# Three edits in a recurrent layer: block transposes for a triangular inverse, a subtraction moved to GpSimd, two projections moved into a norm

## Chip, cores, metric

One NeuronCore of a Trainium2 chip. The metric is the device time of one execution in microseconds. The kernel before: 1786.72 us, median of 3 runs (1777.45 to 1789.82).

## What is computed

Four layers over 512 tokens of width 1024, in float32: an "even" layer (a 31-tap convolution beside an RWKV-7 recurrence), a sparse attention layer, a linear recurrent layer, a second attention layer. Only the even layer is edited. Its recurrence, per head of 64 channels:

```python
def rwkv7_step(state, inp):
    r_t, w_t, k_t, v_t, kk_t, a_t = inp
    sa = jnp.einsum('bhvk,bhk->bhv', state, -kk_t)
    state = (state * w_t[:, :, None, :]
             + sa[..., None] * (kk_t * a_t)[:, :, None, :]
             + v_t[..., None] * k_t[:, :, None, :])
    y = jnp.einsum('bhvk,bhk->bhv', state, r_t)
    return state, y
...
    y = ((y - mu) * lax.rsqrt(var + GN_EPS)).reshape(B, S, RWKV_DIM) * lnx_w + lnx_b
```

Before it, `z = h @ even_w_in` gives all inputs of convolution and recurrence; behind it come a norm per head (the group norm), a gate and `even_w_out`.

## The kernel before, in words

Activations lie transposed, channels on partitions, 512 tokens in the free dimension; a weight tile is 128x128. Every weight product is three matmuls (`mm3`, L166): the weight is split into a high part `wh` and a low part `wl`, the activation into two as well, and L168, L169, L170 add up high x high, high x low and low x high. The split is made in `wparts` (L141): ScalarE writes `wh` (L145) and minus the raw weight, rounded, into `wl` (L146), and an accumulating DMA, issued on GpSimd's queue, adds the raw weight (L147), which leaves the low part. `wsplit` loads and splits one column of 8 tiles; `wrows` (L150) loads, for one input row `k`, the 7 tiles of the first 7 columns, 8 times: 56 tiles. They serve the start (L495 to L506): while the conditioning weights `ada_first` are loaded and multiplied on VectorE (`Ada.columns`, L437: 8 operations of L445 and L447, a matmul L450, and L453, which ends a round), two rows of `h` at a time become ready (L501, L332, L333) and 7 columns accumulate in 7 PSUM banks.

The recurrence runs in two halves of 8 heads, `H0` and `H1`, objects of the class `Half`. `keys` and `prep` make the decayed keys and queries `AR` and `BK`. `inverse` (L658) inverts the 64x64 unit-triangular matrix of each of 8 chunks and 8 heads: L669 makes the products, L671 masks them on VectorE, L672 writes them to DRAM, L675 and L677 read blocks of 32x32 back, so that the row index lies on partitions 32 by 32 (`Nu`) or the upper right block is to hand (`No`). A solve by columns, 108 short operations (54 each of L688 and L689) on VectorE, inverts the diagonal blocks; L690 to L692 spill the result. `merge` (L696) reads it back (L703, L705) and makes the upper right block with two small matmuls per chunk and head (L714, L719). `ahead(c)` (L722) prepares the matrices of the next chunk; it is called for chunk 0 at the end of `inverse`, and its product with the decay (L745) is on GpSimd. `chunk(c)` steps through the 8 chunks and lets 8 steps of an independent projection (`fill`) run in between. `finish` (L804) is the group norm: centring matmuls L811, squares, `head_sums` (L544: L550, the reciprocal root, a transpose L556), then for each of four tiles a broadcast `head_bcast` (L561) and three VectorE operations L827 to L829.

Beside it run the convolution: `conv_in` (two projections), `taps` (27 operations L859 on VectorE, two additions L864 on GpSimd), `conv_stats` (its layer norm: 8 subtractions L888 and 7 additions L894 on GpSimd), `norm_conv`. `yb` is the first half's result, read back and split at L968 to L973 (L972 is a GpSimd subtraction) for 6 columns of `even_w_out`.

The order on each engine is fixed when the program is built: a scheduler with a cost model takes ready instructions by priority, which is the order of the calls; `K.later` lowers the priority, `issue_after(i)` holds an instruction behind `i`. Tiles of one tag share a number of buffers (`s=6`: six), and a new tile waits for the oldest's readers. The order of calls around the change (L919 to L978): `H0.keys`, `H0.prep`, `H0.inverse`, `H0.merge`, `conv_in(3)`, gate projections, `conv_in(4)`, `H1.keys`, the 8 chunks of H0, `H0.finish`, `taps(6)`, `H1.prep` (whose first loop turn projects H1's first `r` and `v`, L613 and L614), `H1.inverse`, later `conv_stats`, `yb`, `norm_conv`, then `H1.merge`.

Of the kernel before, what the change touches and what calls it, by code (L numbers as in the profile page):

```python
# [52 lines left out]
class Ctx:  # L53
# [87 lines left out]
    def wparts(self, raw, tag=None):  # L141

        nc, n = self.nc, raw.shape[1]
        h, l = ((self.t(tag, (P, 4, P), R) if tag else self.wp.tile([P, 4, P], R, name=self.name(z), tag=z, bufs=4))[:, :n] for z in ("wh", "wl"))
        nc.scalar.copy(h, raw)  # L145
        nc.scalar.mul(l, raw, -1.0)  # L146
        nc.gpsimd.dma_start(out=l, in_=raw, accum_op=OP.add)  # L147
        return h, l

    def wrows(self, key, ct, k):  # L150
# [6 lines left out]
        for o in (0, 4):  # L157
            m = min(4, n - o)
            h, l = self.wparts(raw[:, o:o + m])
# [300 lines left out]
def even_layer(K, ada1):  # L460
# [12 lines left out]
    with K.layer("even", {"mm": (0, 1), "t": (2, 3, 4), "u": (5, 6), "ada": (7,), "py": (7,)}, s=6, k=4, v=4, q4=3, no=1, Yt=1, BKt=2, SAV=2, U=3, cu=2, fg=3, mean=2, awa=1, pa=1):  # L473
# [70 lines left out]
        def head_sums(sqs, f, n=S):  # L544
# [21 lines left out]
        class Half:  # L566
# [91 lines left out]
            def inverse(self):  # L658
# [3 lines left out]
                No, Nu = K.t("no", (P, 4 * NCH, 32)), K.t("q4", (P, 32, 32))  # L662
                n = K.name("sp")
                nd = K.dram.tile([P, 4 * NCH, C], F, name=n, tag=n)
                for j in range(4):
# [4 lines left out]
                    n = K.t(shape=(P, NCH, C))  # L670
# [7 lines left out]
                Yu, pr = K.t("q4", (P, 32, 32)), K.t("q4", (P, 32, 32))  # L678
# [984 lines left out]
```

## Time and profile before

| what | us |
|---|---|
| median of 3 runs | 1786.72 |
| the profiled execution | 1791.05 |
| its span | 1789.3 |
| PE busy in the span | 1657.9 |
| VectorE (DVE), ScalarE (ACT), GpSimd (POOL) busy | 1142.2, 1090.4, 637.6 |

Engines: PE is TensorE's matmuls, PEld its weight loads, SP the queue that issues most DMAs. A group of instructions is told by its line. "Idle before" is the time its engine did nothing, and behind the arrow stands what ended it. [...]

### The profile page before, as it was taken

Reading aid. Unit: us, or ns where it says so; the run is one execution under the profiler, and the core shown is the slowest. Engines: PE = TensorE matmul, PEld = TensorE weight load, DVE = VectorE, ACT = ScalarE, POOL = GpSimd, SP = SyncE. Lnnn points to the kernel's source line nnn. Section 1 sums busy time; section 2 is a strip of 40 time slices with the busy share of each in tenths; the row PEclk is TensorE's granted clock in tenths of the full one; section 3 lists DMA queues with packets and bytes.
Section 4 is the critical chain, followed back from the end, with each engine's and each line's share of the span. In section 5 each row is a group of like instructions: output and inputs, shape, how many; then the busy total and the mean of one; then the engine's idle time right before and its main releaser. Section 6 shows DMA issues by size and latency. Waiting matters only on the chain.

```text
span 1789.3 us, 26544 instructions
## 1 busy us (share of the span) xinstructions
PE 1657.9 (93%) x9250; PEld 1310.1 (73%) x9250; DVE 1142.2 (64%) x2247; ACT 1090.4 (61%) x2106; POOL 637.6 (36%) x678
## 2 busy tenths in 40 slices
PE   5899999998995999888999899999999999999997
PEld 4676777776664777767887688888788777877775
DVE  6489776795948567456968878922688621454442
ACT  3574545445554435478565678765789755776775
POOL 1244423233566212133323445332333333333332
PEclk9899997898998989899999999999999999999999
DMA  9866894446678976476879741078777798865654
GB/s 284 211 147 163 184 215 110 107 95 174 153 179 193 273 219 151 119 170 142 179 168 229 197 89 35 18 166 193 165 177 167 150 190 190 199 143 138 154 109 116
DMA packets 164087, 289.19 MB, mean 162 GB/s; under 512 B 43985, under 2 KB 60753, under 8 KB 162929
## 3 DMA queue, kind: packets, MB, share of 16 engines
q0 software_dynamic: 60352, 107.24, 35.7%
q1 hardware_dynamic: 99568, 172.91, 30.9%
q10 hardware_dynamic: 4032, 7.34, 1.1%
q8 instruction: 73, 1.20, 0.3%
q14 instruction: 62, 0.50, 0.1%
HBM read 162.10 MB, written 18.12 MB: 101 GB/s over the span
## 4 chain that ended last, share of the span: by engine, by line
PE 59%; DVE 13%; DMA 12%; issue 8%; ACT 3%; POOL 3%; SPq 1%; POOLq 0%; DVEq 0%; ACTq 0%
PE ps L168 15%; PE ps L169 15%; PE ps L170 15%; DVE x L859 4%; DMA wl<-wr 3%; DMA wr<-in_even_w_in 2%; POOL wl L147 1%; DMA adm<-in_ada_w 1%; PE ps L1525 1%; PE ps L729 1%; DMA sp<-gt 1%; PE ps L1521 1%; PE ps L550 1%; PE ps L1261 1%; POOL mean L894 1%
## 5 line engine op out<-in xcount | busy, mean ns | idle before, releaser
L147 POOL DMA_DIRECT2D wl<-wr x416 | 364.7, 882 | 871.6 <-ACT wl L146 772.3
L170 PE MATMUL ps<-h,wl 128*128 128x512 f32 x1240 | 498.8, 406 | 29.4 <-DMA wl<-wr 29.0
L168 PE MATMUL ps<-h,wh 128*128 128x512 f32 x1240 | 508.5, 415 | 18.7 <-ACT h L332 6.8
L169 PE MATMUL ps<-h,wh 128*128 128x512 f32 x1240 | 500.0, 405 | 0.1
L145 ACT CAST wh<-wr 128x512 fp32r<-128x512 f32 (+1 forms) x416 | 251.9, 606 | 355.6 <-PE ps L169 253.8
L170 PEld LDWEIGHTS ps<-h,wl 128*128 128x128 f32 x1240 | 241.0, 195 | 91.0 <-DMA wl<-wr 37.5
L168 PEld LDWEIGHTS ps<-h,wh 128*128 128x128 f32 x1240 | 243.4, 197 | 83.3 <-ACT h L332 8.3
L169 PEld LDWEIGHTS ps<-h,wh 128*128 128x128 f32 x1240 | 242.0, 195 | 52.7 <-issue 2.7
L146 ACT ACTIVATE wl<-wr 128x512 fp32r<-128x512 f32 (+1 forms) x416 | 256.5, 617 | 28.0 <-PE ps L169 26.5
L859 DVE SCALAR_TENSOR_TENSOR x<-cu,vec,x 128x512 f32<-128x512 f32 x216 | 185.9, 862 | 4.9
L1258 POOL TENSOR_SCALAR pp<-pp,st 128x512 f32<-128x512 f32 x32 | 52.2, 1632 | 68.9 <-DVE st L1254 58.8
L1253 ACT ACTIVATE pp<-pp,st 128x512 f32<-128x512 f32 x64 | 46.2, 722 | 18.2 <-DVE st L1252 18.0
L1515 DVE CUSTOM_DVE_ANT_0 pp<-ps,nb 128x128 f32<-128x128 f32 (+3 forms) x64 | 30.6, 488 | 30.3 <-PE ps L1510 21.8
L169 PE MATMUL ps<-wl,h 128*128 128x512 f32 x120 | 47.6, 398 | 0.7 <-DMA wl<-wr 0.7
L1252 DVE CUSTOM_DVE_ANT_0 pp<-ps,bias 128x512 f32<-128x512 f32 x64 | 43.6, 681 | 6.4 <-PE ps L1261 6.0
L170 PE MATMUL ps<-wh,h 128*128 128x512 f32 x120 | 46.5, 393 | 0.0
L688 DVE TENSOR_TENSOR q<-q,q 128x112 f32<-128x112 f32 (+25 forms) x108 | 27.2, 288 | 29.2 <-DMA q<-sp 28.8
L168 PE MATMUL ps<-wh,h 128*128 128x512 f32 x120 | 45.4, 405 | 0.0
L288 ACT CAST pT<-ps 128x512 fp32r<-128x512 f32 x64 | 36.4, 577 | 14.1 <-PE ps L1261 13.6
L1518 POOL TENSOR_SCALAR pp<-pp,st 128x128 f32<-128x128 f32 (+1 forms) x32 | 32.0, 1032 | 36.5 <-DVE st L1517 36.4
L289 DVE TENSOR_TENSOR pT<-ps,pT 128x512 fp32r<-128x512 f32 x64 | 43.3, 680 | 0.8 <-ACT pT L288 0.7
L1188 DVE MATCH_REPLACE8 acc<-m,acc 128x512 f32<-128x512 f32 x64 | 42.8, 674 | 0.0
(522 smaller groups left out, 3332.1 us busy)
## 6 DMA issues: line engine op xcount, KB each, us to landing
wl<-wr POOLq DMA_DIRECT2D x376, 256.0 KB, 4.1
wr<-in_even_w_in SPq DMA_DIRECT2D x50, 512.0 KB, 4.1
wr<-in_odd_w_in SPq DMA_DIRECT2D x39, 512.0 KB, 4.2
wr<-in_lru_w_in SPq DMA_DIRECT2D x24, 512.0 KB, 3.8
wr<-in_fox_w_qkg SPq DMA_DIRECT2D x24, 512.0 KB, 4.4
k<-in_ada_w SPq DMA_DIRECT2D x32, 256.0 KB, 3.9
wr<-in_odd_w_out SPq DMA_DIRECT2D x16, 512.0 KB, 4.0
wl<-wr POOLq DMA_DIRECT2D x40, 192.0 KB, 4.1
```

What stands on the lines that cost most here:

```text
L145: nc.scalar.copy(h, raw)
L146: nc.scalar.mul(l, raw, -1.0)
L147: nc.gpsimd.dma_start(out=l, in_=raw, accum_op=OP.add)
L168: mm(ps, lhsT=w[0], rhs=x[0], start=first, stop=False)
L169: mm(ps, lhsT=w[0], rhs=x[1], start=False, stop=False)
L170: self.last_mm = mm(ps, lhsT=w[1], rhs=x[0], start=False, stop=last).ins
L289: nc.vector.tensor_tensor(out=l, in0=src, in1=h.bitcast(F), op=OP.subtract)
L859: nc.vector.scalar_tensor_tensor(out=acc, in0=u[:, q:q + S], scalar=w[q], in1=acc, op0=OP.mult, op1=OP.add)
L1188: nc.vector.match_replace(out=acc, in_to_replace=m8, in_values=acc, imm_value=TAKEN)
L1252: nc.vector.tensor_tensor_reduce(out=pp, in0=lg, in1=bias[t], scale=1.0, scalar=3e38, op0=OP.add, op1=OP.min, accum_out=mx)
L1253: nc.scalar.activation(pp, pp, AF.Exp, scale=-1.0, bias=mx, accum_out=sm)
L1258: (nc.vector if t % 2 else nc.gpsimd).tensor_scalar(out=pp, in0=pp, scalar1=sm, scalar2=None, op0=OP.mult)
```

## The change

`wparts` gets a flag: with it, GpSimd subtracts `wh` from the raw weight directly. Only `wrows` sets it. `inverse` keeps the unmasked products in `Yt` (ScalarE copies) and turns 32x32 blocks with VectorE's transpose, before and after the solve; no DRAM is used, `No` goes. `ahead(0)` moves from the end of `inverse` into `merge`. `ahead`'s decay product goes to four ScalarE multiplications. `conv_in(3)` is called ahead of `H0.merge`. In `H0.finish`, H1's first `r` projection is called inside `head_sums` and its first `v` projection behind it, with the transposes and broadcasts held behind their last matmuls; `H1.prep` then finds them done. L894 moves to VectorE. The split of `yb` goes the other way: from a GpSimd subtraction to ScalarE and an accumulating DMA.

```diff
     def wparts(self, raw, tag=None, sub=False):
         nc.scalar.copy(h, raw)
-        nc.scalar.mul(l, raw, -1.0)
-        nc.gpsimd.dma_start(out=l, in_=raw, accum_op=OP.add)
+        if sub:
+            nc.gpsimd.tensor_tensor(out=l, in0=raw, in1=h.bitcast(F), op=OP.subtract)
+        else:
+            nc.scalar.mul(l, raw, -1.0)
+            nc.gpsimd.dma_start(out=l, in_=raw, accum_op=OP.add)
...
-            h, l = self.wparts(raw[:, o:o + m])
+            h, l = self.wparts(raw[:, o:o + m], sub=True)
...
-        def head_sums(sqs, f, n=S):
+        def head_sums(sqs, f, n=S, behind=None):
...
+            if behind:
+                behind()
             p = K.ps("t")
-            for t in range(nt):
-                nc.tensor.transpose(p[:16, t * P:(t + 1) * P], hl[:, t].bitcast(F), K.ident)
+            with K.tc.issue_after(K.last_mm) if behind else contextlib.nullcontext():
+                for t in range(nt):
+                    nc.tensor.transpose(p[:16, t * P:(t + 1) * P], hl[:, t].bitcast(F), K.ident)
...
+                Yt = self.Yt = K.t("Yt", (P, 4 * NCH, C))
                 for j in range(4):
...
-                    nc.vector.tensor_tensor(out=n, in0=v3(p), in1=gmask[:, None, 0:C].to_broadcast([P, NCH, C]), op=OP.mult)
-                    nc.sync.dma_start(out=nd[:, NCH * j:NCH * j + NCH], in_=n)
-                quarters = [(b, q, 64 * b + 32 * q, slice(64 * q + 32 * b, 64 * q + 32 * b + 32)) for b in range(2) for q in range(2)]
-                for b, q, r, o in quarters:
-                    nc.sync.dma_start(out=Nu[o], in_=nd[r:r + 32, :, 32 * q:32 * q + 32].rearrange("a u b -> u a b"))
-                    if q == 0:
-                        nc.sync.dma_start(out=No[r:r + 32], in_=nd[r:r + 32, :, 32:64])
+                    nc.scalar.copy(Yt[:, NCH * j:NCH * j + NCH], v3(p))
+                quarters = [(q, slice(64 * b + 32 * q, 64 * b + 32 * q + 32)) for q in range(2) for b in range(2)]
+                turn = nc.vector.transpose
...
+                for q, r in [(0, slice(0, P))] + quarters[2:]:
+                    turn(out=Nu[r].rearrange("u a b -> u b a"), in_=Yt[r, :, 32 * q:32 * q + 32].rearrange("a u b -> a b u"))
...
-                Yd = K.spill(Yu)
-                self.last = nc.vector.tensor_copy(pr[0:64], Yu[0:64].rearrange("p a b -> p b a"))
-                Xd = K.spill(pr[0:64])
+                X11 = self.X11 = K.t("q4", (P, 32, 32))
+                turn(out=X11.rearrange("p u a -> p a u"), in_=Yu)
+                for q, r in quarters[2:] + [(0, slice(0, P))]:
+                    self.last = turn(out=Yt[r, :, 32 * q:32 * q + 32].rearrange("p u b -> p b u"), in_=Yu[r].rearrange("u a b -> u b a"))
+
+            def merge(self, fill=()):
...
+                for b in range(2):
+                    nc.gpsimd.memset(Yt[64 * b + 32:64 * b + 64, :, 0:32], 0.0)
                 self.ahead(0, K.t("SAV", (P, 2, 4, C)))
...
-                    nc.gpsimd.tensor_tensor(out=bk, in0=BK[:, :, c].rearrange("p j a t -> p j (a t)"), in1=pcb, op=OP.mult)
                     p = K.ps("t")
                     for j in range(4):
+                        nc.scalar.mul(bk[:, j], BK[:, j, c].rearrange("p a t -> p (a t)"), self.PC[:, j, c:c + 1])
                         nc.tensor.transpose(p[:, j * P:(j + 1) * P], bk[:, j], K.ident)
...
-                r8 = head_sums(sqs, f_gn, n)
+                r8 = head_sums(sqs, f_gn, n, behind[0])
+                if behind[1]:
+                    behind[1]()
+                after = K.last_mm if behind[1] else None
                 for j, (y, ft) in enumerate(zip(ys, self.fts)):
-                    p = head_bcast(r8, j)
+                    with K.tc.issue_after(after) if after else contextlib.nullcontext():
+                        p = head_bcast(r8, j)
...
-                    nc.gpsimd.tensor_tensor(out=acc, in0=acc, in1=sq[:, :S], op=OP.add)
+                    nc.vector.tensor_tensor(out=acc, in0=acc, in1=sq[:, :S], op=OP.add)
...
+        conv_in(3)
         H0.merge()
-        conv_in(3)
...
-        H0.finish(gates)
+        H0.finish(gates, behind=(lambda: K.project(W, [CR + 4], hT, H1.ev_r), lambda: K.project(W, [CVV + 4], hT, H1.ev_v)))
...
                 nc.scalar.copy(h, y)
-                nc.gpsimd.tensor_tensor(out=l, in0=y, in1=h.bitcast(F), op=OP.subtract)
+                nc.scalar.mul(l, y, -1.0)
+                nc.gpsimd.dma_start(out=l, in_=y, accum_op=OP.add)
```

## Rows read from the trace of the kernel before

**Rows 1.** Windows (start:end, length, busy us per engine, PEclk, DMA share, GB/s).
```profile
0.00:785.00 785.00, 688.26 (x4556) 530.51 (x4556) 551.96 (x967) 386.75 (x721) 278.38 (x296) 0.91 0.71 176
785.00:1789.00 1004.00, 969.60 (x4694) 779.56 (x4694) 590.19 (x1281) 703.61 (x1386) 359.25 (x382) 0.99 0.66 150
214.00:285.00 71.00, 64.84 (x411) 52.16 (x409) 46.08 (x144) 33.72 (x63) 21.38 (x24) 0.90 0.94 202
412.00:440.00 28.00, 23.52 (x89) 15.11 (x88) 11.47 (x18) 14.04 (x24) 4.63 (x6) 0.78 0.76 198
440.00:517.00 77.00, 69.02 (x357) 49.18 (x356) 62.80 (x80) 39.52 (x68) 40.65 (x42) 0.90 0.62 147
517.00:600.00 83.00, 64.76 (x466) 51.42 (x464) 53.21 (x134) 43.06 (x75) 51.08 (x40) 0.86 0.91 227
```

**Rows 2.** Waits of PE, 0 to 780 us (total, times, longest).
```profile
PE ps L170 <- DMA wl<-wr: 23.0, 9, 10.9
```

**Rows 3.** DMA queues, 0 to 80 us (packets, MB, share).
```profile
q1 hardware_dynamic: 11360, 17.09, 64.9%
q0 software_dynamic: 2304, 3.67, 27.0%
```

**Rows 4.** Timeline of VectorE, the first stage (start, duration, idle before).
```profile
22.95 0.16 DVE L453 TENSOR_TENSOR mod<-ps,vec 128x4 f32<-128x4 f32 x1 [1.96 <-PE ps L450]
35.66 0.16 DVE L453 TENSOR_TENSOR mod<-ps,vec 128x4 f32<-128x4 f32 x1 [3.09 <-PE ps L450]
...
70.47 0.16 DVE L453 TENSOR_TENSOR mod<-ps,vec 128x4 f32<-128x4 f32 x1 [2.56 <-PE ps L450]
```

**Rows 5.** Lines of GpSimd, 0 to 785 us (busy, mean ns, idle before).
```profile
L864 POOL TENSOR_TENSOR pa<-pa,awa 128x512 f32<-128x512 f32 x16 | 25.4, 1589 | 15.2 <-ACT awa L863 14.9
...
L745 POOL TENSOR_TENSOR s<-BK,PC 128x512 f32<-128x512 f32 x14 | 15.8, 1233 | 5.6 <-PE ps L719 5.4
L888 POOL TENSOR_TENSOR x<-x,mean 128x512 f32<-128x512 f32 x8 | 10.0, 1277 | 0.1
```

**Rows 6.** Lines of VectorE and ScalarE, 0 to 785 us.
```profile
L447 DVE SCALAR_TENSOR_TENSOR SAV<-AR,cs,SAV 128x512 f32<-128x512 f32 x14 | 10.5, 749 | 2.3 <-DMA AR<-in_ada_first 1.9
...
L904 DVE RECIPROCAL mean<-mean 128x512 f32<-128x512 f32 x1 | 3.4, 3353 | 4.6 <-ACT mean L899 4.6
...
L750 ACT COPY BKt<-ps 128x512 f32<-128x512 f32 x14 | 8.1, 580 | 4.6 <-PE ps L748 3.1 <-PE ps L790 1.3
...
L801 ACT COPY AR<-ps 128x256 f32<-128x256 f32 x16 | 6.0, 373 | 6.6 <-PE ps L800 6.5
```

**Rows 7.** Timelines of VectorE and PE, the inverse of H0.
```profile
230.29 0.28 DVE L688 TENSOR_TENSOR q<-q,q 128x31 f32<-128x31 f32 x2 [15.89 <-DMA q<-sp]
...
251.55 0.18 DVE L689 TENSOR_TENSOR q<-q,q 128x8 f32<-128x8 f32 x1
...
252.84 1.11 DVE L691 COPY q<-q 64x1024 f32<-64x1024 f32 x1
...
270.87 3.59 PE L714 MATMUL ps<-q,no 32*32 32x32 f32 x64 [3.15 <-issue]
```

**Rows 8.** Timelines of ScalarE and PE, the group norm of H0.
```profile
434.24 0.69 ACT L527 ACTIVATE s<-ps,tiny 128x512 f32<-128x512 f32 x1 [6.33 <-DVE AR L829]
...
436.78 0.79 PE L168 MATMUL ps<-h,wh 128*128 128x512 f32 x1 [2.43 <-DVE s L528]
```

**Rows 9.** Timelines of GpSimd, VectorE and PE, the inverse of H1.
```profile
511.16 9.99 POOL L888 TENSOR_TENSOR x<-x,mean 128x512 f32<-128x512 f32 x8
...
530.40 1.38 DVE L688 TENSOR_TENSOR q<-q,q 128x31 f32<-128x31 f32 x2 [12.87 <-DMA q<-sp]
...
537.26 12.65 POOL L894 TENSOR_TENSOR mean<-mean,cu 128x512 f32<-128x512 f32 x1
...
554.89 0.79 PE L170 MATMUL ps<-h,wl 128*128 128x512 f32 x1 [10.93 <-DMA wl<-wr]
...
581.38 3.59 PE L714 MATMUL ps<-q,no 32*32 32x32 f32 x64 [5.82 <-issue]
```

More of the change, by code (lines that the diff above doesn't have):

```diff
@@ L139, in wsplit, with wparts @@
         return out
-    def wparts(self, raw, tag=None):
+    def wparts(self, raw, tag=None, sub=False):
         nc, n = self.nc, raw.shape[1]
@@ L472, in even_layer @@
     A = Ada(K, 0)
-    with K.layer("even", {"mm": (0, 1), "t": (2, 3, 4), "u": (5, 6), "ada": (7,), "py": (7,)}, s=6, k=4, v=4, q4=3, no=1, Yt=1, BKt=2, SAV=2, U=3, cu=2, fg=3, mean=2, awa=1, pa=1):
+    with K.layer("even", {"mm": (0, 1), "t": (2, 3, 4), "u": (5, 6), "ada": (7,), "py": (7,)}, s=6, k=4, v=4, q4=3, Yt=1, BKt=2, SAV=2, U=3, cu=2, fg=3, mean=2, awa=1, pa=1):
         xT, hT = [], []
@@ L669, in inverse @@
                             mm(p[hs(b), c * C:(c + 1) * C], lhsT=BK[hs(b), j, c, b], rhs=AR[hs(b), j, c, 0], start=True, stop=True)
[L670 to L678 removed]
+                    nc.scalar.copy(Yt[:, NCH * j:NCH * j + NCH], v3(p))
+                quarters = [(q, slice(64 * b + 32 * q, 64 * b + 32 * q + 32)) for q in range(2) for b in range(2)]
+                turn = nc.vector.transpose
+                Nu, Yu, pr = (K.t("q4", (P, 32, 32)) for _ in range(3))
                 nc.gpsimd.memset(Yu, 0.0)
                 nc.gpsimd.memset(Yu.rearrange("p a b -> p (a b)")[:, 0::33], 1.0)
+                for q, r in [(0, slice(0, P))] + quarters[2:]:
+                    turn(out=Nu[r].rearrange("u a b -> u b a"), in_=Yt[r, :, 32 * q:32 * q + 32].rearrange("a u b -> a b u"))
                 for b in range(31):
@@ L689, in inverse @@
                             eng.tensor_tensor(out=Yu[:, a, b + 1:], in0=Yu[:, a, b + 1:], in1=z, op=OP.add)
-                Yd = K.spill(Yu)
-                self.last = nc.vector.tensor_copy(pr[0:64], Yu[0:64].rearrange("p a b -> p b a"))
-                Xd = K.spill(pr[0:64])
-                self.ahead(0, K.t("SAV", (P, 2, 4, C)))
-                self.parts = No, Yd, Xd, quarters
-            def merge(self, fill=()):
-                No, Yd, Xd, quarters = self.parts
-                Yt = self.Yt = K.t("Yt", (P, 4 * NCH, C))
-                X11 = K.t("q4", (P, 4 * NCH, 32))
-                for b, q, r, o in quarters:
-                    f = lambda d, o: d[o].rearrange("u a b -> a u b")
-                    nc.sync.dma_start(out=Yt[r:r + 32, :, 32 * q:32 * q + 32], in_=f(Yd, o))
-                    if q == 0:
-                        nc.sync.dma_start(out=X11[r:r + 32], in_=f(Xd, o))
-                    else:
-                        nc.gpsimd.memset(Yt[r:r + 32, :, 0:32], 0.0)
+                X11 = self.X11 = K.t("q4", (P, 32, 32))
[3 more added lines that the diff above has]
+            def merge(self, fill=()):
+                Yt, X11 = self.Yt, self.X11
+                for b in range(2):
+                    nc.gpsimd.memset(Yt[64 * b + 32:64 * b + 64, :, 0:32], 0.0)
+                self.ahead(0, K.t("SAV", (P, 2, 4, C)))
                 for u in range(0, 4 * NCH, 16):
@@ L713, in merge @@
                         for c in range(16):
-                            i = mm(p[r2, 32 * c:32 * c + 32], lhsT=No[r, u + c], rhs=X11[r, u + c], start=True, stop=True)
+                            i = mm(p[r2, 32 * c:32 * c + 32], lhsT=Yt[r, u + c, 32:64], rhs=X11[r, u + c], start=True, stop=True)
                         if fill:
@@ L802, in chunk, with finish @@
                 return last.ins
-            def finish(self, gate, c0=0, c1=NCH):
+            def finish(self, gate, c0=0, c1=NCH, behind=(None, None)):
                 n = (c1 - c0) * C
```

4 lines of the change are left out of this document (removed).

## Prediction

> **What bounds the kernel now.** Read the stage windows first [rows 1]. From 785 us on nothing is edited; TensorE (PE) is busy there 969.60 of 1004 us at a granted clock of 0.99, so there is nothing to win. The first 785 us are the edited layer: PE is busy 688.26 us, idle 97 us, and the mean clock is 0.91. [...] Second, the waits of PE [rows 2]: the largest sum is for `wl`, the low half of a weight, 23.0 us in nine waits. Third, the timelines, which place the rest: four places, taken in order of time.
>
> **Place 1: the first 56 weight tiles (`wrows`).** Up to 80 us the DMA engines move loads for 64.9% of the time and accumulating DMAs, which make `wl` from `wr`, for 27.0%, 21.6 us [rows 3]; together 92%. The 16 accumulating DMAs of `wrows` become 16 GpSimd subtractions, and 16 ScalarE multiplications go. The stage's pace is read at L453, which ends each of the four rounds of `Ada.columns`: the first at 22.95 us, the second at 35.66, the fourth at 70.47 [rows 4]. The first interval, 12.71 us, is a round that waits for no DMA; the other two are 17.4 on average. With the loads alone (52 us of DMA time) all intervals could be 12.71: the last round ends at 22.95 + 3 x 12.71 = 61.1, 9.4 us earlier. That is the upper end.
> What GpSimd's subtraction costs is not shown for this place; the nearest rows are its other 128x512 operations [rows 5]: 1277 ns alone (L888), 1589 ns beside the taps on VectorE (L864). Sixteen of them (half are 128x384) need about 22 us of some 50, and GpSimd has nothing else there. But both engines hold each other up: if each of the four subtractions of an interval keeps VectorE from its chain (L447, 749 ns each [rows 6]) for 1277 ns, an interval is 12.71 + 5.1 us, and the last round ends at 22.95 + 53.4 = 76.4, 5.9 us later than now. That is the lower end, -6. VectorE waits for DMA or PE in a part of each round, so I take a quarter of that delay, 1.3 us an interval: gain 9.4 - 3.9, say **5 us** (-6 to 9).
> [...]
>
> **Place 2: the inverse of the first half (H0).** Now the masked blocks go to DRAM and come back transposed: VectorE stands idle 15.89 us before the solve starts at 230.29; the solve ends at 251.7; after it a spill, a second round trip, and the merge's matmuls start at 270.87 after a PE wait of 3.15 [rows 7]. Per inverse 4 masking multiplications, 18 DMAs and a strided copy go; 4 ScalarE copies (about 0.58 us, as L750 [rows 6]) and 7 VectorE block transposes of 1024 elements per partition come: 3 before the solve, 4 after. No row shows such a transpose. Below it lies the strided copy of 1024 elements after this solve, 1.11 us (L691) [rows 7], above it the slowest VectorE operation, the reciprocal, 3353 ns for 512 elements, so 6.7 us for 1024 [rows 6]. I take 1.2 us, near the copy, since it moves and doesn't compute. So the chain from last block product to merge loses 15.89 + 19.1 = 35 us of waiting and gets 7 x 1.2 + about 1.5 for copies and memset = 10: 25 us shorter. That is not 25 us of time, because PE works on independent projections meanwhile. The window 214 to 285 has PE busy 64.84 of 71 us: 6.2 idle; its clock of 0.90 means 14 us at half speed, of which about 10 with work, 5 us of it lost [rows 1]. Ceiling 11. What is late next is the supply of independent projections, which now must also fill the earlier chunks. I take **6 us** (0 to 11). `conv_in(3)` moved ahead of the merge is such a filler: nothing.
>
> **Place 3: the group norm of H0 (`finish`).** 412 to 440 has 4.5 us idle at 0.78 [rows 1], which is 12 us at half speed; about 9 of them with work, 4.5 lost. Ceiling 9. The largest wait, 2.43 us, is for the evacuation of H1's first `r` projection, whose ScalarE half itself waited 6.33 us for the norm's last step (L829) to free a tile [rows 8]. Issued ahead of the norm's own tiles, that wait goes. But the scheduler already put one of the two projections into this stretch (4.5 of 28 us idle is all that is left), and the two that move are not extra work; `head_bcast` now queues behind 24 of their 48 matmuls on PE, and the norm's chain behind it, which only the next stage reads. I take **4 us** (0 to 9).
>
> **Place 4: the inverse of H1.** The dearest. VectorE idles 12.87 us, from 517.5 to the solve's start at 530.40. Inside it one of GpSimd's L894 holds its queue from 537.26 for 12.65 us; behind it in that queue stand the issues of `wl` DMAs, and PE idles 10.93 us for `wl` until 554.89; then 5.82 us more until the merge at 581.38 [rows 9]. The window 517 to 600: 18.2 us idle, clock 0.86, 23 us at half speed of which about 11 with work: 5.6 lost [rows 1]. Ceiling 24. The change takes L894's seven additions to VectorE (about 0.7 us each, 5 us, before or behind the solve) and the four subtractions of `yb` off GpSimd (four accumulating DMAs and four ScalarE multiplications instead), so nothing that reads SBUF should be queued on GpSimd during the solve. Left is L888, eight subtractions of 1277 ns [rows 5], which ran from 511.16 to 521.15 [rows 9] and must end before the solve begins: with three transposes after 517.5, at about 521. If they don't, the queue is blocked for the whole solve, 21.4 us (230.29 to 251.7) instead of 12.65, PE stalls 9 us longer, and only the merge wait of 6 goes: -3. I take **15 us** (-3 to 24).
>
> **The rest.** `ahead`'s product moves from GpSimd (1233 ns, L745 [rows 5]) to four ScalarE multiplications of 128 columns. From 373 ns for 256 columns and 580 for 512 [rows 6] one is about 270 ns: 1.1 us, as long as before, 15 us over 14 chunks on an engine that is busy 387 of 785 us [rows 1]. It stands ahead of the copies of U in ScalarE's queue, but PE has filler there: 0 (-3 to 3).
>
> **Sum.** 5 + 6 + 4 + 15 = 30 us. The profiled execution took 1791.05 us (span 1789.3), 4.3 above the median of 1786.72. 1791.05 - 30 = 1761, and less 4.3: **1757 us**, 1.7% under the median. About 1% (18 us, below 1769 or above 1805) is what a measurement of this kernel can tell from no change.
>
> **Rivals.**
> *A, the stall stays at H1.* L888 overlaps the earlier solve, or PE has no filler: place 4 gives 3 instead of 15, the sum is 18: 1769. For it: L888 ended at about 521, just where the solve would begin. [...]
> *B, the lock bites in the first stage.* Place 1 gives -6: sum 19, 1768. For it: VectorE's chain is the stage's pacemaker. Against: it idles in each round, and the two intervals above 12.71 were long for the DMAs that now go.
> *C, the waits come back elsewhere.* The filler is used up early or late all the same, and the preparation of H1 runs at VectorE's pace (62.80 of 77 us between 440 and 517 [rows 1]): places 2 to 4 give a third of 25, place 1 its 5: 13, so 1773. It includes that the two moved projections change nothing.
> *D, slower: a dear transpose.* At the reciprocal's rate, 6.7 us, seven of them and the 1.5 make 48.4 us, 13 more than the 35 they replace, in each inverse; PE has run out of filler there already, so both times 13 us are PE's: 26 - 5 - 4 = 17 us more, 1804. From 4.8 us a transpose the chain is no shorter; from about 5.5 the whole is slower than before.
>
> **Chances.** Forecast 0.56, A 0.14, B 0.09, C 0.14, D 0.07. Nearly all of the forecast and a part of A and B lie under 1769, so faster by over 1% has 0.63. D and what lies beyond it give slower by over 1% 0.07, and within 1% is left 0.30. The range: the four ceilings add up to 53 (1734), all at once unlikely: 1736 below; above it takes in A, B and C with some room and stops short of D: 1786.
>
> **What would show it.** In the profile after: L453's last row near 65 us, no DMA of `software_dynamic` kind before 70; VectorE's idle time before the solves under 6 us; transposes near 1.2 us; no L894 on GpSimd and no PE wait near 10 us for `wl`; waits in 412 to 440 under 2 us; window 0 to 785 ending near 755. Wrong if transposes take over 4 us, if GpSimd's subtractions in the first stage mean over 2.5 us, or if idle time of PE in the layer stays near 97 us.

## The result, and the profile after

The changed kernel takes 1758.93 us (median of 4 runs, 1758.11 to 1759.96), the kernel before 1786.72: a ratio of 0.9854 over the single runs (0.9844 by the medians), 95% interval 0.9826 to 0.9882. The forecast was 1757. The profiled execution took 1759.96 us, its span 1758.1. In the changed file the lines from L141 on stand 4 further down (L453 is L457), those of `inverse` and behind it shift a little more; all numbers below are those of the changed file unless a row of before is meant.

The windows of the changed kernel that answer to [rows 1] (PEclk is the granted TensorE clock as a share of full speed); where a stage became shorter, its window did too:

```profile
0.00:754.00 754.00, 678.54 (x4551) 523.26 (x4551) 571.68 (x974) 399.76 (x769) 249.84 (x274) 0.93 0.66 171
214.00:285.00 71.00, 68.31 (x534) 56.48 (x533) 66.20 (x159) 38.11 (x67) 21.39 (x25) 0.94 0.72 165
400.00:443.00 43.00, 39.12 (x161) 28.30 (x159) 20.97 (x30) 23.12 (x41) 12.24 (x13) 0.92 0.71 179
443.00:511.00 68.00, 57.96 (x293) 38.28 (x294) 55.50 (x66) 33.67 (x59) 37.01 (x35) 0.82 0.50 126
511.00:573.00 62.00, 57.44 (x396) 45.52 (x397) 55.04 (x139) 44.07 (x87) 20.95 (x23) 0.94 0.92 230
```

The edited layer ends 31 us earlier in the profiled execution; between the medians the gain is 28 us, as the profiled execution of before lay 4.3 us above its median and that of the changed kernel 1.0. Behind the layer, from 754 to 1758 us, TensorE works 969.16 of 1004 us, as before. In the layer TensorE's idle time fell from 97 to 75.5 us and its mean clock rose from 0.91 to 0.93. The window around the first inverse lost 3.5 us of its idle time, the one around the second inverse fell from 83 to 62 us. One row went the wrong way: the preparation of H1 (443 to 511) now has 10 us of idle time at a clock of 0.82, where it had 8 at 0.90.

TensorE's largest wait in the layer is one at its very start that the change doesn't touch (L364 for VectorE's L356, 12.8 us; 12.1 before). The rows behind it say what is late now; the 23.0 us for `wl` of [rows 2] are 8.2:

```profile
PE ps L172 <- ACT h L336: 8.9, 4, 2.7
PE ps L656 <- DVE s L651: 8.9, 3, 4.7
PE ps L174 <- DMA wl<-wr: 8.2, 7, 2.5
```

**Where the time came from, by stage.** I add up, from windows of some 4 us, TensorE's idle time and half of the time in which it worked at a granted clock of 0.50, as the prediction did for single places. TensorE is the layer's busiest engine in both kernels (688.26 of 785 us before, 678.54 of 754 after; no other is above 552 and 572). Its clock has two levels in the trace: of 1570 windows of 0.5 us in the layer of before, 1274 have 1.00, 262 have 0.50, and 34 lie between. At 0.50 its 128x512 products started every 0.43 us (298.85 to 300.99 us), at 1.00 every 0.23 (301.36 to 301.82). "Control" is a second profile of the changed kernel. The sums are estimates (they shrink by 38 and 40 us where the layer got 31 and 33 shorter), so they rank the stages and don't measure them. The border of two stages alone is worth some 4 us: cut exactly at the first and the last chunk step, H1's inverse keeps 7.8 and 7.7 us and its steps 12.3 and 12.9.

| stage | before | after | control |
|---|---|---|---|
| start and H0's keys and prep (0 to 200 us) | 43.7 | 44.0 | 40.8 |
| H0's inverse and merge | 11.6 | 7.1 | 8.1 |
| H0's eight chunk steps | 18.5 | 8.2 | 6.8 |
| group norm and H1's prep | 23.5 | 25.3 | 25.3 |
| H1's inverse and merge | 24.4 | 9.3 | 13.3 |
| H1's eight chunk steps | 18.3 | 9.8 | 6.3 |
| rest of the layer | 9.4 | 7.6 | 8.6 |
| end of the layer (last L989, L990), us | 766.1 | 734.8 | 732.7 |

Some 20 of the 38 us were lost before in the chunk steps, a stage for which the prediction's only term was the 0 of the decay product. The windows of these steps, first half and second half, of before (285 to 404, 600 to 721) and after (285 to 388, 572 to 691):

```profile
285.00:404.00 119.00, 113.72 (x1087) 91.18 (x1084) 98.20 (x139) 54.96 (x112) 43.80 (x49) 0.89 0.39 97
600.00:721.00 121.00, 111.79 (x1029) 88.63 (x1028) 81.50 (x163) 51.83 (x116) 23.02 (x29) 0.92 0.69 191
```
```profile
285.00:388.00 103.00, 99.01 (x956) 78.22 (x955) 83.97 (x124) 57.35 (x130) 35.74 (x41) 0.96 0.44 108
572.00:691.00 119.00, 112.23 (x1095) 89.30 (x1095) 84.04 (x168) 58.91 (x135) 23.84 (x30) 0.94 0.75 217
```

TensorE was nearly always busy in the first one before, too (5 us idle), but at a mean clock of 0.89. The granted clock was 0.50 for some 14 us behind a stall of 2.9 us, for some 3 us behind one of 1.9 us, and for some 10 us from 291 on without a stall ahead of it: in the 6 us before, TensorE was busy all the time, for a good part with products of 32 and of 2 columns (L719, L550). So an idle stretch stood ahead of two of these three stretches only; what lowered the clock is not shown.

**Place 1 after.** The DMA queue that made `wl` is at 0.3% instead of 27.0% of 0 to 80 us, and the subtractions cost 1.4 and 1.2 us. But the rounds end at 39.36 and 69.10, against 35.66 and 70.47 in [rows 4]. DMA queues, GpSimd's lines and the rounds:

```profile
q0 software_dynamic: 22, 0.05, 0.3%
```
```profile
L148 POOL TENSOR_TENSOR wl<-wr,wh 128x512 fp32r<-128x512 f32 x8 | 11.2, 1398 | 33.4 <-ACT wh L146 33.4
L148 POOL TENSOR_TENSOR wl<-wr,wh 128x384 fp32r<-128x384 f32 x8 | 9.9, 1234 | 2.5 <-ACT wh L146 1.3 <-PE ps L174 1.2
```
```profile
39.36 0.16 DVE L457 TENSOR_TENSOR mod<-ps,vec 128x4 f32<-128x4 f32 x1 [3.89 <-PE ps L454]
53.45 0.16 DVE L457 TENSOR_TENSOR mod<-ps,vec 128x4 f32<-128x4 f32 x1 [2.35 <-PE ps L454]
69.10 0.16 DVE L457 TENSOR_TENSOR mod<-ps,vec 128x4 f32<-128x4 f32 x1 [6.10 <-PE ps L454]
```

Each round waits for TensorE's L454, and the last one 6.10 us. (The rounds of before waited for the same products, L450, as the brackets of [rows 4] say; there the third, at 54.81, waited longest, 7.99 us, and in TensorE's queue ahead of its L450 stood products that waited 3.65 us for `wl`.) VectorE had finished the last round's sums at 63.0; L454 ran at 68.11, because it stands in TensorE's queue behind the 42 products of two rows of `h`:

```profile
57.52 5.48 DVE L451 SCALAR_TENSOR_TENSOR SAV<-BK,cs,SAV 128x512 f32<-128x512 f32 x7
```
```profile
68.11 0.95 PE L454 MATMUL ps<-ones,SAV 128*128 128x1 f32 x8
```

GpSimd and VectorE do hold each other up here. The seven operations L451 took 5.48 us in this last round, where the subtractions began only with the last of them, and 7.22 us in the round before, with two subtractions (VectorE, then GpSimd):

```profile
43.88 7.22 DVE L451 SCALAR_TENSOR_TENSOR SAV<-AR,cs,SAV 128x512 f32<-128x512 f32 x7
```
```profile
47.06 2.71 POOL L148 TENSOR_TENSOR wl<-wr,wh 128x512 fp32r<-128x512 f32 x2 [5.71 <-ACT wh L146]
```

That is 1.7 us in one round and 0.9 in another (6.39 us for the seven), about the 1.3 that the prediction took; behind TensorE's order it doesn't show in the rounds' ends.

**The inverses after.** Timelines of VectorE (three transposes before the solve, four behind it) and TensorE in H0:

```profile
210.14 6.75 DVE L683 STREAM_TRANSPOSE q<-Yt 128x1024 f32<-128x1024 f32 x3 [0.20 <-ACT Yt L676]
...
237.93 2.10 DVE L694 STREAM_TRANSPOSE q<-q 128x1024 f32<-128x1024 f32 x1
240.04 7.07 DVE L696 STREAM_TRANSPOSE Yt<-q 32x1024 f32<-32x1024 f32 x3
```
```profile
248.55 1.19 PE L710 MATMUL ps<-q,Yt 32*32 32x32 f32 x32
```

Against [rows 7] the wait before the solve (15.89 us) is gone, the solve starts at 216.9 instead of 230.29, and the merge's first product at 248.55 instead of 270.87. A transpose of 1024 elements takes 2.0 to 2.3 us, on 128 partitions as on 32. Yet the first chunk step (L777) starts at 289.2, against 287.1 before: TensorE had other work either way. In H1 (GpSimd, then VectorE):

```profile
501.15 12.58 POOL L888 TENSOR_TENSOR x<-x,mean 128x512 f32<-128x512 f32 x8
```
```profile
516.98 4.44 DVE L683 STREAM_TRANSPOSE q<-Yt 32x1024 f32<-32x1024 f32 x2
521.45 0.28 DVE L691 TENSOR_TENSOR q<-q,q 128x31 f32<-128x31 f32 x2
```

L888 ends at 513.7, 8 us before the solve; no GpSimd operation but the issuing of DMAs meets the solve, which takes 21.0 us instead of 26.9. The 12.65 us of [rows 9] and TensorE's 10.93 us behind it have no counterpart.

### The profile page after: what moved, and what is told of

Its sections match the earlier page's. It is cut to its first block, busy times and chain, and to the rows that moved or that the text cites. A ratio compares the mean times of both kernels' runs of the same rounds, so it can differ in the third digit from the quotient of the medians.

```text
span 1758.1 us, 26497 instructions
## 1 busy us (share of the span) xinstructions
PE 1647.7 (94%) x9250; PEld 1302.3 (74%) x9250; DVE 1163.9 (66%) x2258; ACT 1105.8 (63%) x2158; POOL 610.0 (35%) x657
## 4 chain that ended last, share of the span: by engine, by line
PE 64%; DVE 14%; DMA 8%; issue 7%; ACT 5%; POOL 2%; SPq 0%; POOLq 0%; ACTq 0%; DVEq 0%
PE ps L172 17%; PE ps L173 17%; PE ps L174 16%; DMA wl<-wr 3%; DVE x L859 3%; PE ps L725 1%; PE ps L1526 1%; DVE q L692 1%; DVE q L691 1%; DMA s<-sp 1%; DMA cu<-sp 1%; PE ps L1522 1%; POOL wl L151 1%; DMA adm<-in_ada_w 1%; PE ps L1262 1%
## 5 line engine op out<-in xcount | busy, mean ns | idle before, releaser
L151 POOL DMA_DIRECT2D wl<-wr x400 | 349.0, 876 | 843.4 <-ACT wl L150 731.2
L150 ACT ACTIVATE wl<-wr 128x512 fp32r<-128x512 f32 (+1 forms) x400 | 247.6, 619 | 29.5 <-PE ps L173 27.0
L859 DVE SCALAR_TENSOR_TENSOR x<-cu,vec,x 128x512 f32<-128x512 f32 x216 | 181.4, 841 | 4.7
L1254 ACT ACTIVATE pp<-pp,st 128x512 f32<-128x512 f32 x64 | 46.2, 722 | 17.6 <-DVE st L1253 17.4
L1523 ACT COPY pT<-ps 128x128 f32<-128x128 f32 (+3 forms) x64 | 25.8, 419 | 27.7 <-PE ps L1522 27.5
```

What stands on the lines that cost most here:

```text
L859: nc.vector.scalar_tensor_tensor(out=acc, in0=u[:, q:q + S], scalar=w[q], in1=acc, op0=OP.mult, op1=OP.add)
L1254: nc.scalar.activation(pp, pp, AF.Exp, scale=-1.0, bias=mx, accum_out=sm)
```

## The experiments

All ratios are to the kernel before, measured on the same chip in between. The control's ratio is 0.9848 (0.982 to 0.9875), so a single ratio says little below 5 us; a difference in us is that of two ratios times 1787, and its interval is 6 to 7 us to either side. The control ran on the chip of the first three experiments; the others ran on two more chips, each beside its own runs of the kernel before. The unedited last 1020 us took 1017 to 1027 in the profiled executions, so the end of the layer in the profile (control 732.7, changed kernel 734.8, mean 733.8) is given beside it; two profiles of one kernel differ by 2 us there.

**Control** (no edit).

> The changed kernel once more, untouched, as the zero of the runs beside it. Expected 1758.9 us, within 2 us. If it differs by more, the runs beside it are compared with this one and not with the first time.

1762.39 us (1750.59 to 1765.98), ratio 0.9848. The spread of a single kernel here is 15 us, eight times that of the four runs above.

**Place 1 undone.**

```diff
-            h, l = self.wparts(raw[:, o:o + m], sub=True)
+            h, l = self.wparts(raw[:, o:o + m])
```

> The changed kernel with the first 56 tiles split by ScalarE and the accumulating DMA again (place 1 undone, nothing else). The prediction's term for this edit was 5 us, so by it this run takes 1764. My theory now: the loads no longer set the pace after the change, but TensorE's order does (L454, four small products that end a round, stands in TensorE's queue behind 42 matmuls of the round before), so the edit won only what the last round's end shows, 70.47 to 69.10: this run is 1 to 2 us slower than the control, 1760 to 1761, and the last row of L457 lies at about 70.5. Rival: GpSimd and VectorE held each other up (rival B of the prediction): this run is faster than the control, down to 1753.

Ratio 0.9833 (0.9806 to 0.9861), 3 us less than the control: no difference that can be told. The profile shows the edit where it acts: without it the last round ends at 74.0 instead of 68.1 and 69.1, and the layer at 735.9 instead of 733.8. So the subtraction wins 5 us at the end of the start (the expectation had 70.5 for this round, not 74.0), and at most 2 of them are left at the layer's end, no more than two profiles of one kernel differ by. The 5 us term was too large; that the engines' holding each other up makes the kernel slower (rival B) doesn't show.

**TensorE's order in the start.** `K.last_col` is the last L454.

```diff
-            for p, w in zip(pss, ws[i]):
-                K.mm3(p, w, hT[i], i == 0, i == ND - 1)
+            with K.tc.issue_after(K.last_col) if i % 2 and i < 7 else contextlib.nullcontext():
+                for p, w in zip(pss, ws[i]):
+                    K.mm3(p, w, hT[i], i == 0, i == ND - 1)
```

> The changed kernel with one line of order added in the start: the 21 matmuls of each odd row of h are issued behind L454, the products that end a round, so that these no longer wait in TensorE's queue behind work that nobody waits for. If TensorE's order is what limits the start after the change, the last round's mod (L457) comes at 63 to 65 us instead of 69.10, TensorE's 2 us waits for h in each round shrink, and the kernel takes 1752 to 1755. Rival: TensorE's amount of work, or VectorE's chain, is the limit there, and the order changes nothing: within 1 us of the control.

Rounds of this kernel:

```profile
49.58 0.16 DVE L457 TENSOR_TENSOR mod<-ps,vec 128x4 f32<-128x4 f32 x1 [1.21 <-PE ps L454]
64.73 0.17 DVE L457 TENSOR_TENSOR mod<-ps,vec 128x4 f32<-128x4 f32 x1 [2.02 <-PE ps L454]
```

The order was what held the rounds: they end at 49.58 and 64.73, as expected, and the intervals of the second and third are 11.8 and 12.2 us. The last is 15.15, with four of VectorE's eight operations lengthened by 3.3 us in all beside subtractions. But the kernel doesn't get faster, a miss: ratio 0.9862 (0.9834 to 0.9889), end of the layer 735.3. H0's last block product ends at 207.2, against 206.3 in the control and 209.5 in the changed kernel: the gain is gone after the keys and the preparation, between 80 and 200 us, where VectorE is busy 107 of 120 us. That this is also why place 1 won little is likely, but not shown.

**Place 3 undone.**

```diff
-        H0.finish(gates, behind=(lambda: K.project(W, [CR + 4], hT, H1.ev_r), lambda: K.project(W, [CVV + 4], hT, H1.ev_v)))
+        H0.finish(gates)
```

> The changed kernel with the group norm of the first half called plainly; the first r and v projections of the second half come in its preparation again (place 3 undone, nothing else). By the prediction's term, 4 us, this run takes 1763. My theory now: the edit won nothing or cost up to 4 us, because the norm's chain ends later in the changed kernel (443.5 us, while the steps before it end 8 to 10 us earlier) and VectorE's preparation of the second half, 58 of 70 us busy from 430 on, sets the pace behind it: 1755 to 1760. The windows 400:430 and 430:500 show which: TensorE's idle time in both together is 13.9 us in the changed kernel.

Ratio 0.983 (0.9805 to 0.9856), 3 us less than the control, within the noise. The last step of the norm (L829), first in the changed kernel and then here:

```profile
442.82 0.69 DVE L829 TENSOR_TENSOR AR<-AR,s 128x512 f32<-128x512 f32 x1 [0.51 <-DMA s<-sp]
```
```profile
425.30 0.67 DVE L829 TENSOR_TENSOR AR<-AR,s 128x512 f32<-128x512 f32 x1
```

With the edit the norm ends 17.5 us later, because each broadcast (L570) stands behind the two projections, and H1's block products end at 508 to 511 instead of 503.5. Without it the norm and the preparation lose 18.2 us in place of 25.3, but the second half's steps and the rest of the layer lose 29.1 in place of 17.4 and 14.9 (changed kernel and control), and the layer ends at 741.1. So the edit moves loss from one stage to another; which is larger stays open.

**The block transposes alone**, on the kernel before (with `ahead(0)` in `merge`; all else as it was).

```diff
-                    nc.vector.tensor_tensor(out=n, in0=v3(p), in1=gmask[:, None, 0:C].to_broadcast([P, NCH, C]), op=OP.mult)
-                    nc.sync.dma_start(out=nd[:, NCH * j:NCH * j + NCH], in_=n)
...
+                    turn(out=Nu[r].rearrange("u a b -> u b a"), in_=Yt[r, :, 32 * q:32 * q + 32].rearrange("a u b -> a b u"))
...
+                    self.last = turn(out=Yt[r, :, 32 * q:32 * q + 32].rearrange("p u b -> p b u"), in_=Yu[r].rearrange("u a b -> u b a"))
```

> The kernel before with the block transposes in inverse and merge alone (ahead(0) moves into merge with them; no other edit). Theory: besides the shorter chains around both solves (about 8 us in both together) the steps of the chunks get faster, because SyncE's queue no longer holds the loads of the ada weights behind the inverse's round trip, and VectorE no longer waits for them in front of products that TensorE needs: the first half's chunk steps take about 100 us instead of 115, the kernel 15 to 20 us less, 1767 to 1772. Rival: the chunk steps got faster by the decay product's move from GpSimd to ScalarE; then they stay at 115 here, and the kernel takes 1777 to 1780.

1765.14 us, ratio 0.9875 (0.9847 to 0.9903): 22 us less than before, the largest single part; end of the layer 745.2. The first half's chunk steps (from the first L777, L782 before, to the last) take 105.2 us, between 115.3 before and 98.6 after, neither the 100 of the theory nor the 115 of the rival, so part of their gain is here and part elsewhere. The lock at H1 is back (GpSimd, then TensorE; L883 is L894 of before):

```profile
527.41 11.65 POOL L883 TENSOR_TENSOR mean<-mean,cu 128x512 f32<-128x512 f32 x1
```
```profile
544.03 0.80 PE L170 MATMUL ps<-h,wl 128*128 128x512 f32 x1 [9.62 <-DMA wl<-wr]
```

**L894 alone, and L894 undone.** The first on the kernel before, the second on the changed one:

```diff
-                    nc.gpsimd.tensor_tensor(out=acc, in0=acc, in1=sq[:, :S], op=OP.add)
+                    nc.vector.tensor_tensor(out=acc, in0=acc, in1=sq[:, :S], op=OP.add)
```

> The kernel before with one edit of the change alone: the seven additions L894 on VectorE. Theory: GpSimd's 12.65 us lock beside the solve goes, and with it TensorE's 10.93 us wait for wl and 3 us of work at the low clock behind it: 10 to 14 us less than before, 1773 to 1777 against 1787, and no idle time of TensorE above 5 us between 517 and 603. Rival: the four GpSimd subtractions of yb (L972), which this kernel keeps, or the last of L888 take the lock over: less than 4 us won, and another GpSimd operation of about 10 us stands beside the solve.

1780.66 us, ratio 0.9966 (0.9944 to 0.9988): 6 us (2 to 10), half of what was expected; end of the layer 753.6 (before 766.1), 12.5 us, where one profile of each is compared. The 10.93 us wait of TensorE is gone, but the two pairs of L972, still on GpSimd, ran at 545.35 and 549.96 inside the solve, and this took 26.2 us.

```diff
-                    nc.vector.tensor_tensor(out=acc, in0=acc, in1=sq[:, :S], op=OP.add)
+                    nc.gpsimd.tensor_tensor(out=acc, in0=acc, in1=sq[:, :S], op=OP.add)
```

> The changed kernel with L894's seven additions on GpSimd again (nothing else). Theory: the additions start at about 505 us, take 1.3 to 1.7 us each between the subtractions L888, so the last of them meet the solve (521.5 to 542.4) and one is held for 10 us or more; TensorE idles behind the wl transfers in GpSimd's queue and the kernel takes 8 to 13 us more than the control. Rival: they end before the solve now, since it comes no earlier relative to them, or nothing that TensorE needs is queued behind: within 3 us of the control.

1766.24 us, ratio 0.9872 (0.9844 to 0.9899), 4 us more than the control, within the noise; end of the layer 737.7. The 8 to 13 us of the theory didn't come, and no addition was held. Three ran inside the solve (516.8 to 544.2), 1.59 us each, as this one:

```profile
521.57 1.59 POOL L894 TENSOR_TENSOR mean<-mean,cu 128x512 f32<-128x512 f32 x1
```

This time only VectorE paid: its solve took 27.4 us in place of 21.0. In the four kernels with three or more of GpSimd's L894 or L972 beside the second solve, the solve takes 26.2 to 28.5 us. Whether a GpSimd operation is held as well, and TensorE behind it, differs from kernel to kernel, and even within one solve: before, additions at 529.56 and 531.72 passed in 2.1 us each, and the one at 537.26 was held for 12.65.

**The decay product back on GpSimd.**

```diff
-                        nc.scalar.mul(bk[:, j], BK[:, j, c].rearrange("p a t -> p (a t)"), self.PC[:, j, c:c + 1])
+                    nc.gpsimd.tensor_tensor(out=bk, in0=BK[:, :, c].rearrange("p j a t -> p j (a t)"), in1=pcb, op=OP.mult)
```

> The changed kernel with the decay product of ahead on GpSimd again (one operation of 128x512 in place of four on ScalarE; nothing else). Theory: this edit is worth nothing, as predicted; within 3 us of the control, chunk steps of the first half about 99 us, of the second about 118. Rival: it is what made the chunk steps 17 us shorter; then they take 110 to 115 here, and the kernel 1770 to 1777.

1772.94 us, ratio 0.9924 (0.9901 to 0.9947): 14 us more than the control, end of the layer 752.8. My theory, and the prediction's 0, fall; the rival holds (its steps of 110 to 115 are 109.3). This is what the trace shows there. GpSimd, VectorE and TensorE of this kernel near 300 us:

```profile
298.53 5.37 POOL L741 TENSOR_TENSOR s<-BK,PC 128x512 f32<-128x512 f32 x5
303.57 1.68 POOL L762 TENSOR_TENSOR U<-SAV,PC 64x256 f32<-64x256 f32 x2
```
```profile
298.02 6.74 DVE L858 TENSOR_SCALAR x<-cu,vec,tiny 128x512 f32<-128x512 f32 x1
304.80 0.69 DVE L727 TENSOR_TENSOR q<-ps,gmask 128x512 f32<-128x512 f32 x1
```
```profile
305.55 0.48 PE L725 MATMUL ps<-AR,BK 64*128 64x128 f32 x2 [2.25 <-DVE q L727]
```

The product needs only `BK` and `PC`, so GpSimd runs five chunks' worth ahead, back to back, with two operations more behind: 6.7 us without a gap. (L762 is the decayed state.) The first tap of a convolution on VectorE, L858, 0.55 us in the kernel before (L857), lasts just as long; the masking product L727 stands behind it in VectorE's queue, TensorE waits for L727 (2.25 us), and then its products are slower for a while: the four of L732 take 1.06 us at 308.59, where they took 0.63 at 298.17. The kernel before has a held tap, too (GpSimd, VectorE, TensorE):

```profile
306.20 4.35 POOL L745 TENSOR_TENSOR s<-BK,PC 128x512 f32<-128x512 f32 x4
```
```profile
307.23 4.46 DVE L859 SCALAR_TENSOR_TENSOR x<-cu,vec,x 128x512 f32<-128x512 f32 x1
```
```profile
320.65 0.63 PE L748 MATMUL ps<-ident,s 128*128 128x128 f32 x4 [2.91 <-DVE q L731]
```

Its tap lasted 4.46 us, against a mean of 859 ns of the 83 taps in this stage. TensorE's stall, the one of 2.9 us with some 14 us at a clock of 0.50 behind it, comes later there: VectorE went on without a gap behind the held tap and stood 1.27 us for the load of a conditioning weight before it came to L731, so how much of that stall is the tap's is not shown. The four kernels with the product on GpSimd all have one such operation near 300 us: 4.46 us (before), 4.53 (L894 alone), 6.76 (the transposes alone) and 6.74 (this one). Of the ten others none has a VectorE operation above 2 us among the first half's steps.

**The decay product on VectorE.** Is it the engine that it left, or the place it took in ScalarE's queue?

```diff
-                        nc.scalar.mul(bk[:, j], BK[:, j, c].rearrange("p a t -> p (a t)"), self.PC[:, j, c:c + 1])
+                    nc.vector.tensor_tensor(out=bk, in0=BK[:, :, c].rearrange("p j a t -> p j (a t)"), in1=pcb, op=OP.mult)
```

> The changed kernel with ahead's decay product on VectorE (one operation of 128x512 in place of four on ScalarE). Theory: what the move off GpSimd won is that no train of GpSimd operations holds a VectorE operation any more; five decay products and two more stood back to back for 6.7 us where the product is on GpSimd, and one VectorE operation lasted 6.74 us beside them. So this run has no VectorE operation above 3 us between 285 and 400, chunk steps of the first half of 99 to 102 us, and a time within 4 us of the control. Rival: the order of ScalarE's queue made the difference; then the chunk steps take 107 us or more, and the kernel 8 to 12 us more than the control.

1758.41 us, ratio 0.9836 (0.981 to 0.9863), end of the layer 734.6, first-half steps 98.5 us: as the control. Windows of the chunk steps with the product on GpSimd, then on VectorE:

```profile
285.00:401.00 116.00, 110.14 (x963) 87.17 (x962) 91.37 (x128) 51.04 (x107) 42.35 (x48) 0.88 0.41 98
```
```profile
285.00:387.00 102.00, 100.16 (x957) 78.93 (x956) 87.61 (x131) 50.31 (x106) 36.08 (x41) 0.98 0.44 109
```

What counts is that GpSimd doesn't do it; the place in ScalarE's queue made no difference that can be told.

**A second product on GpSimd that nobody reads.**

```diff
+                    nc.gpsimd.tensor_tensor(out=K.dummy, in0=BK[:, :, c].rearrange("p j a t -> p j (a t)"), in1=self.PC[:, :, c].unsqueeze(2).to_broadcast([P, 4, P]), op=OP.mult)
```

> The changed kernel with the decay product on ScalarE as it is, and the same product once more on GpSimd, written to a tile that nobody reads. Theory: GpSimd's mere activity holds VectorE; one VectorE operation lasts 5 to 7 us near 300 us again, the first half's chunk steps take 105 us or more instead of 99, and the kernel 5 to 12 us more than the control. Rival: it was the wait for GpSimd's result, or the order that came with it; then nothing changes, within 3 us.

1773.19 us, ratio 0.992 (0.9895 to 0.9944): 13 us more than the control, about what the theory wanted, but not at the place it named. With no buffer to wait for, all of them ran ahead, those of H0 from 197 to 208 us and of H1 from 514 to 527, and the first half's steps took 97.2 us as ever. Timelines of GpSimd and VectorE:

```profile
200.43 4.27 POOL L741 TENSOR_TENSOR dummy<-BK,PC 128x512 f32<-128x512 f32 x3
...
205.37 2.82 POOL L741 TENSOR_TENSOR dummy<-BK,PC 128x512 f32<-128x512 f32 x2
```
```profile
198.89 8.40 DVE L861 SCALAR_TENSOR_TENSOR x<-cu,vec,x 128x512 f32<-128x512 f32 x5
...
209.26 3.89 DVE L861 SCALAR_TENSOR_TENSOR x<-cu,vec,x 128x512 f32<-128x512 f32 x5
```

Beside them five taps took 8.40 us, the next five without them 3.89, and the first step came 3 us later. Most of the 13 us were lost in H1, whose steps end at 703.1 instead of 688.3 in the control: the solve, with two of the products inside it, takes 23.4 us in place of 21.0, and how the rest is lost is open. (The length of H1's steps, 128.3 us instead of 118.4, says little: the run with the product on VectorE has 130.4 and loses nothing.) So GpSimd's work costs time though nobody waits for its result; the train near 300 us rests on the two runs before this one.

**Each transpose twice.**

```diff
-                turn = nc.vector.transpose
+                def turn(out, in_):
+                    nc.vector.transpose(out=out, in_=in_)
+                    return nc.vector.transpose(out=out, in_=in_)
```

> The changed kernel with each of the seven block transposes of an inverse done twice (same result). At 2.0 to 2.3 us each the chain around each solve gets 15 us longer, 30 us in both. Theory: TensorE has other work beside most of it; in the first half, whose first step came no earlier than before although its merge came 17 us earlier, it costs 0 to 3 us, in the second 5 to 9: 5 to 12 us more than the control. Rival: by the arithmetic of rival D of the prediction TensorE has run out of filler there and all of it is lost: 25 to 30 us more.

1780.65 us, ratio 0.9963 (0.9939 to 0.9986): 21 us more than the control, end of the layer 753.2, 19 more. Between the two theories: of the 14 added transposes (31 us at 2.24 each) two thirds are TensorE's. The first half, for which the theory had 0 to 3 us, costs 8 to 10: its steps end at 395.6 instead of 387.8 and 385.6 (changed kernel and control). One wait in H1 has 8.6 us of it, since G's masking product stands behind the transposes in VectorE's queue:

```profile
564.44 1.12 PE L745 MATMUL ps<-ident,s 128*128 128x128 f32 x4 [8.57 <-DVE q L729]
```

**The bonus product later.** A try to win the 8.9 us wait for L651.

```diff
-                        for f in pending:
-                            f(K.last_mm)
-                        pending = []
+                        for f in pending[:-1]:
+                            f(K.last_mm)
+                        pending = pending[-1:]
...
-                for f in pending:
-                    f(K.last_mm)
+                self.pending = pending
...
+                for f in self.pending:
+                    f(i.ins)
```

> The changed kernel with each bonus product (L656, which waits for VectorE's L651) issued one projection later in TensorE's order, and the last two behind the products of the inverse. Theory: TensorE's waits for L651, 8.9 us in three, go, and some of the low clock behind them: 4 to 8 us less than the control. Rival: VectorE's pace sets the preparation of the second half anyway, and the wait comes back in front of the next projection or of the products L675: within 3 us.

1773.92 us, ratio 0.9923 (0.9896 to 0.9951): 13 us slower, a miss; end of the layer 752.2. TensorE's largest wait from 440 to 515:

```profile
PE ps L656 <- ACT s L545: 7.8, 1, 7.8
```

The waits for L651 went (0.2 us is left), and one as long came for ScalarE's L545 of the next turn. A bonus that is held longer also holds its tiles of tag `s` longer, of which there are six; that this is the reason is not shown. Nor is it where the 13 us went: H1's block products end at 501.2, 7 to 10 us earlier than in the control and the changed kernel. But now the solve begins before GpSimd's eight subtractions (L888, here L889) are done, the overlap that rival A of the prediction had feared (GpSimd, then VectorE; each such pair takes 0.3 us in the changed kernel):

```profile
508.16 10.02 POOL L889 TENSOR_TENSOR x<-x,mean 128x512 f32<-128x512 f32 x8
```
```profile
511.90 2.58 DVE L693 TENSOR_TENSOR q<-q,q 128x31 f32<-128x31 f32 x2
514.40 2.59 DVE L692 TENSOR_TENSOR q<-q,q 128x60 f32<-128x60 f32 x2
```

With these and VectorE's own seven additions inside it the solve takes 32.2 us, and H1's steps end at 707.7 instead of 688.3 and 690.8; how the steps lose the most of it is open.

No run beats the changed kernel by more than the noise. Left as it is, or with the decay product on VectorE or place 1 or 3 undone, it takes the same time.

## Why the prediction came out right, and where not

The total (30 us off the layer; 31 measured between the two profiled executions, 28 between the medians) is right, but in part by luck: its terms are right in two of five, and what places 1 and 3 gave too little was made up by a stage that had no gain in the sum. Two of its signs came out otherwise, the rounds' end (69.10, not near 65) and the transposes (2.24 us, not near 1.2); none of its signs of being wrong came.

- **Place 1, 5 us: too large.** The step that failed is "the last round ends at 61.1" plus a delay by GpSimd. The loads did stop to matter, GpSimd's subtractions took 1.2 to 1.4 us each, and they held VectorE for 0.9 to 1.7 us in a round, about as taken. What the sum had at nothing is TensorE's order: it made the intervals 14.1 to 15.7 us, and with the order changed two of them are 11.8 and 12.2. The last round ended at 69.10. Left at the layer's end: at most 2 us.
- **Place 2, 6 us: about right in size** (11.6 to 7.1 and 8.1 of loss, an estimate), with a term mis-sized inside it: a transpose takes 2.24 us on average, not 1.2. Twice seven of them, 1.04 us dearer each, are 14.6 us of chain, by the doubled run about 10 us of time (an estimate). It stayed well under the break-even of 4.8 us that rival D named. Each transpose here reads or writes with strides of 32 or 64 elements, or both, and no run has one without; why it takes twice the 1.11 us of the strided copy of as many elements [rows 7] is open.
- **Place 3, 4 us: not shown.** The wait for the evacuation of `r` went, as predicted, and the norm's chain, which "only the next stage reads", ended 17.5 us later; that the next stage is then late was not priced. Undoing it changes nothing that can be told.
- **Place 4, 15 us: right** (24.4 to 9.3 and 13.3). GpSimd ends its work 8 us before the solve, so rival A, L888 in the solve, did not come. But the addition was only a part: alone it won 6 by the times, with L972 inside the solve in its place.
- **The rest, 0 (-3 to 3): wrong, and the largest miss.** The decay product's move, an edit beside the three of the title, is worth 14 us by the times and 19 by the layer's end. The prediction priced it by its duration on two engines that had room, and not by what it holds up: that GpSimd and VectorE hold each other, as the L894 of 12.65 us in [rows 9] showed, was applied at places 1 and 4 only. 4.46 us of one tap stood in the trace of before.

The parts don't add up one by one (22 for the transposes and 6 for L894, each alone on the kernel before, and 14 for the decay product, taken out of the changed one, make 42, of 27 for all): I take it that each takes away stalls that another would have taken, which no run shows by itself.

## What to carry to other kernels

Look in the timeline for single operations that last many times their line's mean; a mean of 859 ns hid one of 4.46 us, and the queue behind it fed TensorE. Where GpSimd's work can run far ahead in a block, try it on another engine (14 us here), and ask what VectorE does beside it. A stage's gain counts only if the next stage can use it: 5 us at the end of the start were at most 2 us at the end of the layer.

## What was not expected of the hardware

- GpSimd and VectorE held each other for longer than one instruction: one VectorE operation of 0.55 us lasted 6.74 us beside seven GpSimd operations without a gap, one GpSimd operation, which took 1.26 us alone (L894 of before at 521.11), lasted 12.65 and 11.65 us beside a solve of short VectorE operations (some 54 of them ran during the 12.65 us), and in another kernel three GpSimd operations passed through the solve at 1.59 us while VectorE lost 6.4 us.
- VectorE's block transpose of 1024 float32 elements per partition takes 2.0 to 2.3 us with the strides that this kernel gives it, on 32 partitions as on 128, so one on 32 partitions costs as much as one on all. Means by shape in the changed kernel:

```profile
L696 DVE STREAM_TRANSPOSE Yt<-q 32x1024 f32<-32x1024 f32 x4 | 9.3, 2326 | 0.1
...
L683 DVE STREAM_TRANSPOSE q<-Yt 128x1024 f32<-128x1024 f32 x2 | 4.5, 2254 | 0.2 <-ACT Yt L676 0.2
L694 DVE STREAM_TRANSPOSE q<-q 128x1024 f32<-128x1024 f32 x2 | 4.1, 2036 | 0.1
```

- A ScalarE multiplication of 128 columns with a scale per partition takes 389 ns on average in the changed kernel, not the 270 drawn from 256 and 512 columns. As neighbours overlap, four of them keep ScalarE busy for 1.26 us (17.6 us for 14 fours), no less than GpSimd's single 1.23 us, and it is still the better place:

```profile
L742 ACT ACTIVATE s<-BK,PC 128x128 f32<-128x128 f32 x56 | 17.6, 389 | 5.7 <-DVE BK L648 4.5 <-DMA sp<-s 1.0
```
